# Feature-major projections: 640 tokens as 320 + 320 instead of 384 + 256

## The chip, the cores and the metric

The kernel runs on one core of one Trainium2 chip. The metric is the device time of one execution in microseconds (us): the median of three runs was 1576.16 us, with 1575.84 and 1576.3 as the lowest and highest.

## The reference, cut to what matters

Two layers act on 128 context tokens and 512 latent tokens, 640 rows of width 1024. Each layer has an input projection to 2560 columns, four mixers, an output projection, a layer norm, and a gated ConvFFN with a convolution of width 3 over the tokens.

```python
h = x * (1 + sc_a) + sh_a
qa, ka, va, ub, vb, qc, kc, vc, gcf, gcb, pd = project(h, w_in)
...
mix = jnp.concatenate([y_a, y_b, y_c, y_d], axis=-1) @ w_out
x = layer_norm(alpha * x + g_a * mix, ln_w[0], ln_b[0])
h = x * (1 + sc_f) + sh_f
x = layer_norm(alpha * x + g_f * conv_ffn(h, ffn_up, ffn_conv_w, ffn_conv_b, ffn_down), ln_w[1], ln_b[1])
...
def conv_ffn(h, up, cw, cb, down):
    u = h @ up
    up_ = jnp.pad(u, ((0, 0), (1, 1), (0, 0)))
    u = up_[:, :-2] * cw[0] + up_[:, 1:-1] * cw[1] + up_[:, 2:] * cw[2] + cb
    a, g = jnp.split(u, 2, axis=-1)
    return (jax.nn.silu(a) * g) @ down
```

## The kernel before, in words

The 640 tokens are five tiles of 128: t = 0 is the context, t = 1 to 4 are the latents. Every float32 operand of a large matmul is split into a high part (`hh` for activations, `wh` for weights) and a low part (`hl`, `wl`), and a product is three matmuls: wh·hh, wl·hh, wh·hl. ScalarE makes the high parts, VectorE subtracts to get the low ones.

Three kinds of projection follow from this.

- Feature-major (`fm_mms`, L537 to L550): 128 output features on the partitions, tokens along the free axis. One unit is one block of 128 features. A PSUM bank holds 512 float32 values, so the 640 tokens of a unit are two groups: `GA`, columns 0 to `SPLIT_COL`, and `GB`, the rest (L535). Each group takes 8 values of k by 3 matmuls, 24 in all. A layer has 16 units in the mixers (queries, keys, values of attention, `qc`, `kc`, gates, pool, `ub`) and 44 in the FFN's up-projection, so 120 units in the program.
- Token-major (`tm_mm`, L814 on) for two of the mixers' inputs: 256 columns a matmul. These don't use `SPLIT_COL`.
- Output and down projection (`wo`, `dn`): activations stationary, 512 columns of weights moving, one PSUM bank for each token tile.

The instructions of each engine stand in the order in which the program is written; there is no scheduler. So what stands at the head of an engine's queue holds up all behind it. The places that the prediction speaks of:

- Entry of the FFN (loop over `order`, L1424 on). The five GA groups of the first five units are issued first; the first GB follows when the queue of half-done units is longer than four. Between them stand the transposes of `to_h` (L508 on) for the last two token tiles: tile 3 after the second GA, tile 4 after the third. `to_h` makes `hh` and `hl` of one tile, in two halves of four k each: lower half L529 (ScalarE, hh) and L530 (VectorE, hl), upper half L531 and L532 (both VectorE). A GA group needs the tiles up to column `SPLIT_COL`; a GB group needs the others, down to the upper half of tile 4.
- The convolution on PSUM: `conv_a` for GA (ScalarE L1207, VectorE L1210 four times, L1213), `conv_b` for GB (ScalarE L1220, VectorE L1221, L1223, L1225).
- Entry of the mixers (`mixers`, L1057 on): four GA groups, four GB groups, each of the first three followed by `rope` on VectorE and GpSimd (L708 to L711), then the key splits (L580), both groups of the first `kc` unit, GA of the second, then `query_split` (L589, L590) and the first scores `sc` (L758), then GB of the second `kc` unit.
- Entry of the down projection (L1480 on): the first two k (`FIRST = 2`) are done for some token tiles ahead of the others, because `hh` and `hl` of the first four k (`EARLY = 4`) come in two parts: columns up to `SPLIT_COL` early, the rest (`early_rest`) after the last GB group.

Of the kernel before, what the change touches and what calls it, by code (L numbers as in the profile page):

```python
# [10 lines left out]
AF = mybir.ActivationFunctionType  # L11
# [3 lines left out]
P = 128  # L15
# [13 lines left out]

W = 640  # L30
NT = 5
SPLIT_COL = 384
UW = 664

C_ID, C_BD, C_MASK, C_RELF, C_TRIF, C_RELB, C_TRIB = 0, 128, 256, 896, 1024, 1152, 1280
# [54 lines left out]
def kernel(  # L90
# [6 lines left out]
    V, S, G, T = nc.vector, nc.scalar, nc.gpsimd, nc.tensor  # L97
# [18 lines left out]
    def unit(shape, name="u"):  # L116
        u = up.tile([P, UW], F32, tag="u", name=nm(name))[:, 0:math.prod(shape[1:])]
        if len(shape) == 3:
            u = u.rearrange("p (a b) -> p a b", b=shape[2])
        elif len(shape) == 4:  # L120
            u = u.rearrange("p (a b c) -> p a b c", b=shape[2], c=shape[3])
        return u
# [4 lines left out]
    def bank(n=512, name="m"):  # L127
        return pp.tile([P, 512], F32, tag="m", name=nm(name))[:, 0:n]
# [231 lines left out]
    def gate_tiles(a, gate, h):  # L360
        out = []
        for cnd in range(2):
            g = unit([P, 512], name="gate")
            side(out=g, in_=a.scratch[gate, cnd, h * 512:(h + 1) * 512].partition_broadcast(P))
            out.append(g)
        return out
# [14 lines left out]
    def params_tiles():  # L381
        return (par.tile([P, 38], F32, tag="prm", name=nm("prm")),
                par.tile([P, 4, 44], F32, tag="cwT", name=nm("cwT")))

    def params2(rc, prm, cwT):
        rows, cr = rc
        pt = bank(name="prT")
        T.transpose(pt[:, 0:38], rows[0:38, :], ident[0:38, 0:38])
        T.transpose(pt[:, 128:216], cr[0:88, 0, :], ident[0:88, 0:88])
        T.transpose(pt[:, 256:344], cr[0:88, 1, :], ident[0:88, 0:88])  # L390
        V.tensor_copy(out=prm, in_=pt[:, 0:38])
        V.tensor_copy(out=cwT[:, 0:2, :], in_=pt[:, 128:216].rearrange("p (t f) -> p t f", t=2))
        V.tensor_copy(out=cwT[:, 2:4, :], in_=pt[:, 256:344].rearrange("p (t f) -> p t f", t=2))
# [27 lines left out]
    def load_res(src, h, only=None, dma=None):  # L421
        for t in range(NT) if only is None else (only,):
            x = unit([P, 512], name="xr")
            (dma or side)(out=x, in_=src(t)[:, h * 512:(h + 1) * 512])
            xs[t, h] = x

    def gated(t, ps, gates):
        tmp = unit([P, 512], name="rt")
        V.tensor_tensor(out=tmp, in0=ps, in1=gates[cond_of(t)], op=ALU.mult)
        return tmp  # L430
# [33 lines left out]
    def normalize(t):  # L464
        r, nb = rn.pop(t)
        for h in range(2):
            S.activation(out=xs[t, h], in_=xs[t, h], func=AF.Identity, scale=r, bias=nb)
# [16 lines left out]
    def ln_bcast(l, i):  # L484
        out = []
        for src in (ln_w, ln_b):
            hs = []
            for h in range(2):
                u = unit([P, 512], name="lnb")
                side(out=u, in_=src[l, i, h * 512:(h + 1) * 512].partition_broadcast(P))  # L490
                hs.append(u)
            out.append(hs)
        return out

    def ln_scale(lnwb):
        for hs in lnwb:
            for u in hs:
                G.tensor_scalar(out=u, in0=u, scalar1=ALPHA, scalar2=None, op0=ALU.mult)
# [35 lines left out]

    GA, GB = (0, SPLIT_COL), (SPLIT_COL, W)  # L535

# [15 lines left out]
    def fm_mm(u, lo, hi):  # L552
        return fm_mms([u], lo, hi)[0]
# [434 lines left out]
    def pool_in(ps_a, ps_b):  # L988
        x = unit([P, 664], name="px")
        for a, b in ((0, 8), (136, 144), (656, 664)):  # L990
            G.memset(x[:, a:b], 0.0)
        S.activation(out=x[:, 8:136], in_=ps_a[:, 0:P], func=AF.Copy)
        S.activation(out=x[:, 144:400], in_=ps_a[:, P:SPLIT_COL], func=AF.Copy)
        S.activation(out=x[:, 400:656], in_=ps_b, func=AF.Copy)
        return x

    def pool_mix(m, prm, pt, x):
# [42 lines left out]
    def tick():  # L1040
        flush()
        if late:
            late.pop(0)()
        for ln in list(lanes):
            while ln:
                try:
                    next(ln[0])
                    break
                except StopIteration:
                    ln.pop(0)  # L1050
                    if ln:
                        continue
                    break
            if not ln:
                lanes.remove(ln)

    def mixers(l, m, prm, mid=None, then=None):  # L1057
# [8 lines left out]
        def start_a(*ii, mid=None, then=None):  # L1066
# [5 lines left out]
            for i, ps in zip(ii, pss):  # L1072
                S.activation(out=raws[i][:, 0:SPLIT_COL], in_=ps, func=AF.Copy)

        def start_b(i):
            ps = fm_mm(us[i], *GB)
            S.activation(out=raws[i][:, SPLIT_COL:W], in_=ps, func=AF.Copy)
            if i < 3:
# [28 lines left out]
        def keep(o):  # L1107
            u = ws.take()
            ps = fm_mm(u, *GA)
            S.activation(out=o[:, 0:SPLIT_COL], in_=ps, func=AF.Copy)  # L1110
            tick()
            ps = fm_mm(u, *GB)
            V.tensor_copy(out=o[:, SPLIT_COL:W], in_=ps)
            ws.free()
# [235 lines left out]
    for l in range(DEPTH):  # L1350
# [106 lines left out]
        def prep(i):  # L1457
            if i < len(steps):
                k = steps[i][1]
                act_split(k, 0, W)  # L1460
# [4 lines left out]
        def dmm(ps, t, k):  # L1465
            c0 = tcol(t)
            wh, wl = us[k // 2]
            s_ = k % KD
            T.matmul(ps, hh[:, s_, c0:c0 + P], wh[:, k % 2, :], start=(k == 0), stop=False)  # L1469
            T.matmul(ps, hh[:, s_, c0:c0 + P], wl[:, k % 2, :], start=False, stop=False)  # L1470
            T.matmul(ps, hl[:, s_, c0:c0 + P], wh[:, k % 2, :], start=False, stop=(k == KF - 1))  # L1471

        for h in range(2):
            pss = [bank(name="dn") for _ in range(NT)]
            us = {}
            cut = KF if h == 0 else KF - TAIL
            for k in range(KF):
                if k % 2 == 0:
                    us[k // 2] = ws.take()
                if k >= cut or k < FIRST - 1:  # L1480
                    continue
                if k == FIRST - 1:
                    for ts in (range(3), range(3, NT)):
                        for kk in range(FIRST):
                            for t in ts:
                                dmm(pss[t], t, kk)
                else:
                    for t in range(NT):
                        dmm(pss[t], t, k)
                if h == 0 and k == KF - 1:  # L1490
                    tmps = [gated(t, pss[t], gates) for t in range(2)] + [None] * 3
                if k % 2 == 1:
                    ws.free()
                while done < min(len(steps), h * KF + k + 1 + AHEAD):
                    prep(done)
                    done += 1
                if h == 1 and owed:
                    owed.pop(0)()
                if h == 1 and k == 7 and nxt:
                    prm2, cwT2 = params_tiles()  # L1500
                    params2(rc, prm2, cwT2)
                if h == 1 and k == 9:
                    gates = gate_tiles(adas[l], 1, 1)
                    load_res(lambda t, x=xd: x[t], 1)
                if h == 1 and k == 11:
                    lnb = ln_bcast(l, 1)
                if h == 1 and k == cut - 1 and nxt:
                    ln_scale(lnb)
            while h == 1 and done < len(steps):
                prep(done)  # L1510
                done += 1
            if h == 0:
                owed = [lambda t=t, ps=pss[t], g=gates, x=tmps[t]: resid(t, 0, ps, g, True, x) for t in range(NT)]
                owed.pop(0)()
                owed.pop(0)()
                continue
            for t in range(NT):
                for k in range(cut, KF):
                    dmm(pss[t], t, k)
                    if nxt and k == cut + 1:  # L1520
                        if t > 1:
                            to_h(t - 2, sb)
                        if t > 0:
                            normalize(t - 1)
                resid(t, 1, pss[t], gates, True)
                if nxt:
                    norm(t)
                else:
                    norm_out(t, lnb, y_out)
                if t == NT - 1:  # L1530
                    ws.free(4)
# [33 lines left out]
```

## Time and profile before

| What | Value |
|---|---|
| Median of three runs | 1576.16 us |
| The profiled execution | 1575.2 us, of which 1573.4 us are its span |
| Matmuls on TensorE | 1535.4 us busy, 98% of the span |
| Weight loads on TensorE | 1353.3 us, 86% |
| VectorE | 962.5 us, 61% |
| ScalarE | 618.0 us, 39% |
| GpSimd | 423.3 us, 27% |
| Mean granted clock of TensorE | 0.991 of full speed |

Busy time of TensorE is no measure of how near it is to its limit, since matmuls are pipelined and one is entered as longer than the distance to the next. The distance from start to start in the timeline is what one more matmul costs. The time of the profiled execution is 0.96 us below the median of the runs.

### The profile page before, as it was taken

The page shows a single profiled execution, that of the slowest core. Times are in us where ns is not written, and L with a number is a line of the kernel's source. Part 1 is how long each engine was busy: PE and PEld are TensorE (multiplying, and loading weights), DVE is VectorE, ACT ScalarE, POOL GpSimd, SP SyncE. Part 2 cuts the span into 40 slices and gives each one's busy share as a digit, 9 for nine tenths or more (in the row PEclk, how much of TensorE's full clock was granted, in tenths as well). Part 3 has the DMA queues.
Part 4 walks back from the last instruction along what each step waited for, and adds up shares of the span by engine and source line. Part 5 has one row for each costly group of instructions (what it writes and reads, how often), then busy time and mean ns, then how long its engine had stood idle before and what let it go on. Part 6 is the DMA issues. An engine that isn't in the chain of part 4 may idle for free.

```text
span 1573.4 us, 24493 instructions
## 1 busy us (share of the span) xinstructions
PE 1535.4 (98%) x9708; PEld 1353.3 (86%) x9708; DVE 962.5 (61%) x1864; ACT 618.0 (39%) x994; POOL 423.3 (27%) x486
## 2 busy tenths in 40 slices
PE   6999999999999999999997999999999999999997
PEld 1988868899999999988787898688999999997885
DVE  3775355786556555745578853657866656674456
ACT  2644453343333333533345344624433333343331
POOL 2402266054101101201127313732541101010104
PEclk9999999999999999999999999999999999999999
DMA  9544416145343443334215323161332221224311
GB/s 336 161 161 151 138 54 201 59 143 187 114 155 114 156 137 132 114 110 132 89 57 180 137 78 107 55 201 55 121 108 81 81 80 55 81 83 139 125 43 67
DMA packets 117791, 187.99 MB, mean 119 GB/s; under 512 B 11492, under 2 KB 77854, under 8 KB 117677
## 3 DMA queue, kind: packets, MB, share of 16 engines
q1 hardware_dynamic: 109517, 163.03, 31.1%
q0 software_dynamic: 8160, 23.40, 4.8%
q8 instruction: 76, 1.25, 0.3%
q14 instruction: 38, 0.31, 0.1%
HBM read 175.35 MB, written 11.04 MB: 118 GB/s over the span
## 4 chain that ended last, share of the span: by engine, by line
PE 88%; DVE 4%; POOL 3%; DMA 2%; issue 1%; ACT 1%; SPq 0%; POOLq 0%; ACTq 0%; DVEq 0%
PE fm L547 18%; PE fm L549 17%; PE fm L548 17%; PE dn L1470 6%; PE dn L1471 6%; PE dn L1469 6%; PE ada L233 2%; PE wo L1379 2%; PE wo L1381 2%; PE wo L1380 2%; DMA st<-in_w_ada_dram 1%; PE PT L794 1%; PE po L809 1%; PE tm L819 1%; PE tm L821 1%
## 5 line engine op out<-in xcount | busy, mean ns | idle before, releaser
L547 PE MATMUL fm<-hh,wh 128*128 128x256 f32 (+1 forms) x1920 | 601.0, 313 | 1.6 <-ACT hh L1299 1.6
L549 PE MATMUL fm<-hl,wh 128*128 128x256 f32 (+1 forms) x1920 | 594.5, 310 | 2.9 <-DVE hl L1304 2.0
L548 PE MATMUL fm<-hh,wl 128*128 128x256 f32 (+1 forms) x1920 | 594.0, 309 | 0.0
L246 DVE TENSOR_TENSOR wl<-st,wh 128x1024 fp32r<-128x1024 f32 x186 | 282.8, 1527 | 178.5 <-ACT wh L245 177.8
L547 PEld LDWEIGHTS fm<-hh,wh 128*128 128x128 f32 x1920 | 363.2, 189 | 30.4 <-ACT cv L1220 11.7
L549 PEld LDWEIGHTS fm<-hl,wh 128*128 128x128 f32 x1920 | 362.6, 189 | 4.8 <-DVE hl L1304 3.0
L548 PEld LDWEIGHTS fm<-hh,wl 128*128 128x128 f32 x1920 | 363.0, 189 | 0.1
L245 ACT ACTIVATE wh<-st 128x1024 fp32r<-128x1024 f32 x188 | 196.3, 1053 | 211.4 <-PE dn L1470 141.9
L1210 DVE SCALAR_TENSOR_TENSOR cv<-fm,cwT,cv 128x127 f32<-128x127 f32 x352 | 122.0, 408 | 109.5 <-ACT cv L1207 109.4
L1470 PE MATMUL dn<-wl,hh 128*128 128x512 f32 x440 | 175.1, 398 | 0.0
L1469 PE MATMUL dn<-wh,hh 128*128 128x512 f32 x440 | 173.7, 395 | 0.0
L1471 PE MATMUL dn<-wh,hl 128*128 128x512 f32 x440 | 173.1, 394 | 0.3 <-DVE hl L1406 0.2
L1207 ACT ACTIVATE cv<-fm,cwT 128x384 f32<-128x384 f32 x88 | 58.9, 673 | 204.2 <-PE fm L549 188.6
L1419 POOL TENSOR_TENSOR act<-cv,cv 128x640 f32<-128x640 f32 x28 | 45.6, 1630 | 301.2 <-DVE cv L1225 233.6
L1220 ACT ACTIVATE cv<-fm,cwT 128x255 f32<-128x255 f32 x88 | 49.6, 564 | 175.9 <-PE fm L549 175.9
L1471 PEld LDWEIGHTS dn<-wh,hl 128*128 128x128 f32 x440 | 82.6, 188 | 20.8 <-DVE hl L1406 1.1
L1469 PEld LDWEIGHTS dn<-wh,hh 128*128 128x128 f32 x440 | 82.6, 188 | 20.8
L1470 PEld LDWEIGHTS dn<-wl,hh 128*128 128x128 f32 x440 | 82.6, 188 | 19.1
L1419 POOL TENSOR_TENSOR y<-cv,cv 128x640 f32<-128x640 f32 x16 | 26.8, 1678 | 182.8 <-DVE cv L1225 182.8
L1221 DVE SCALAR_TENSOR_TENSOR cv<-fm,cwT,bnd 128x1 f32<-128x1 f32 x88 | 19.1, 217 | 89.1 <-ACT cv L1220 89.0
L1379 PE MATMUL wo<-wh,hh 128*128 128x512 f32 x160 | 64.6, 404 | 0.0
L450 POOL TENSOR_TENSOR r<-ve,mhalf 128x1 f32<-128x1 f32 x20 | 16.5, 826 | 177.4 <-DVE neg L456 177.1
(290 smaller groups left out, 2083.9 us busy)
## 6 DMA issues: line engine op xcount, KB each, us to landing
st<-in_ffn_up_dram SPq DMA_DIRECT2D x44, 1024.0 KB
wa<-in_w_ada_dram SPq DMA_DIRECT2D x80, 512.0 KB
st<-in_ffn_down_dram SPq DMA_DIRECT2D x88, 256.0 KB
st<-in_w_in_dram SPq DMA_DIRECT2D x20, 1024.0 KB
st<-in_w_ada_dram SPq DMA_DIRECT2D x16, 512.0 KB
xd<-xr SPq DMA_DIRECT2D x30, 256.0 KB
xr<-xd POOLq DMA_DIRECT2D x30, 256.0 KB, 5.6
st<-in_w_out_dram SPq DMA_DIRECT2D x24, 256.0 KB
```

The lines of the kernel that those rows point to most:

```text
L245: S.activation(out=oh, in_=view, func=AF.Copy)
L246: eng.tensor_tensor(out=ol, in0=view, in1=of, op=ALU.subtract)
L547: T.matmul(ps, wh[:, k, :], hh[:, k, lo:hi], start=(k == 0), stop=False)
L548: T.matmul(ps, wl[:, k, :], hh[:, k, lo:hi], start=False, stop=False)
L549: T.matmul(ps, wh[:, k, :], hl[:, k, lo:hi], start=False, stop=(k == KD - 1))
L1207: S.activation(out=o[:, 0:n], in_=ps, func=AF.Identity, scale=cwT[:, 1, f:f + 1], bias=cwT[:, 3, f:f + 1])
L1210: V.scalar_tensor_tensor(out=o[:, a + d:b - 1 + d], in0=ps[:, a + 1 - d:b - d], scalar=cwT[:, tap, f:f + 1], in1=o[:, a + d:b - 1 + d], op ...
L1379: T.matmul(ps, hh[:, k, c0:c0 + P], wh[:, k % 2, :], start=(k == 0), stop=False)
L1419: G.tensor_tensor(out=dst, in0=a, in1=g, op=ALU.mult)
L1469: T.matmul(ps, hh[:, s_, c0:c0 + P], wh[:, k % 2, :], start=(k == 0), stop=False)
L1470: T.matmul(ps, hh[:, s_, c0:c0 + P], wl[:, k % 2, :], start=False, stop=False)
L1471: T.matmul(ps, hl[:, s_, c0:c0 + P], wh[:, k % 2, :], start=False, stop=(k == KF - 1))
```

## The change: what it does, and the diff

`SPLIT_COL` becomes 320. Every GA and GB group is then 320 columns wide; 960 matmuls each of L547, L548 and L549 lose 64 columns and 960 each gain 64. The instructions on PSUM change in the same way: copies, gates, `conv_a` (its latent piece has 192 columns instead of 256) and `conv_b` (320 instead of 256). Token tile 2, columns 256 to 384, now lies in both groups. So the down projection takes two token tiles first instead of three, since only tiles 0 and 1 are complete in the early part. The pool mixer's copies get their columns from `SPLIT_COL`.

```diff
-SPLIT_COL = 384
+SPLIT_COL = 320
...
         S.activation(out=x[:, 8:136], in_=ps_a[:, 0:P], func=AF.Copy)
-        S.activation(out=x[:, 144:400], in_=ps_a[:, P:SPLIT_COL], func=AF.Copy)
-        S.activation(out=x[:, 400:656], in_=ps_b, func=AF.Copy)
+        S.activation(out=x[:, 144:16 + SPLIT_COL], in_=ps_a[:, P:SPLIT_COL], func=AF.Copy)
+        S.activation(out=x[:, 16 + SPLIT_COL:656], in_=ps_b, func=AF.Copy)
...
-                    for ts in (range(3), range(3, NT)):
+                    for ts in (range(2), range(2, NT)):
```

No instruction is added or removed on any engine. On TensorE, at the entry of layer 1's FFN, the end of the fifth GA group (`fm_10857`) and the start of the first GB group (`fm_10896`) before:

```order
L548 MATMUL fm_10857<-hh,wl_10660 128x384
L549 MATMUL fm_10857<-hl,wh_10659 128x384
L547 MATMUL fm_10896<-hh,wh_10337 128x256
L548 MATMUL fm_10896<-hh,wl_10338 128x256
L549 MATMUL fm_10896<-hl,wh_10337 128x256
```

And the same place of the changed kernel, on TensorE:

```order
L548 MATMUL fm_10857<-hh,wl_10660 128x320
L549 MATMUL fm_10857<-hl,wh_10659 128x320
L547 MATMUL fm_10896<-hh,wh_10337 128x320
L548 MATMUL fm_10896<-hh,wl_10338 128x320
L549 MATMUL fm_10896<-hl,wh_10337 128x320
```

Nothing moved there; only the widths differ. The one move is on TensorE at the entry of the down projection, here of layer 0 (`dn_6677` to `dn_6681` are the banks of token tiles 0 to 4):

```order
 L1470 MATMUL dn_6678<-wl_6395,hh 128x512
 L1471 MATMUL dn_6678<-wh_6394,hl 128x512
-L1469 MATMUL dn_6679<-wh_6394,hh 128x512
-L1470 MATMUL dn_6679<-wl_6395,hh 128x512
-L1471 MATMUL dn_6679<-wh_6394,hl 128x512
 L1469 MATMUL dn_6677<-wh_6394,hh 128x512
 L1470 MATMUL dn_6677<-wl_6395,hh 128x512
```

The three matmuls of k = 0 for token tile 2 now stand behind those of k = 1 for tiles 0 and 1, so 12 matmuls come ahead of the first that needs the late part, where it was 18.

## Rows read from the trace of the kernel before

**Rows 1.** The page: busy time of the engines; the chain that ended last.

```profile
PE 1535.4 (98%) x9708; PEld 1353.3 (86%) x9708; DVE 962.5 (61%) x1864; ACT 618.0 (39%) x994; POOL 423.3 (27%) x486
...
PE 88%; DVE 4%; POOL 3%; DMA 2%; issue 1%; ACT 1%; SPq 0%; POOLq 0%; ACTq 0%; DVEq 0%
```

**Rows 2.** Groups of instructions by shape, TensorE: count, busy us and mean ns, idle.

```profile
L547 PE MATMUL fm<-hh,wh 128*128 128x384 f32 x960 | 328.7, 342 | 1.6 <-ACT hh L1299 1.6
...
L547 PE MATMUL fm<-hh,wh 128*128 128x256 f32 x960 | 272.3, 284 | 0.0
```

**Rows 3.** Timeline, TensorE, one up-projection unit of layer 0: start us, us, instruction, [idle before].

```profile
455.05 0.28 PE L547 MATMUL fm<-hh,wh 128*128 128x256 f32 x1
...
457.90 0.34 PE L547 MATMUL fm<-hh,wh 128*128 128x384 f32 x1
...
462.07 0.28 PE L547 MATMUL fm<-hh,wh 128*128 128x256 f32 x1
```

**Rows 4.** Timeline, TensorE, the down projection of layer 0, 24 matmuls apart.

```profile
689.89 0.39 PE L1469 MATMUL dn<-wh,hh 128*128 128x512 f32 x1
...
695.49 0.39 PE L1469 MATMUL dn<-wh,hh 128*128 128x512 f32 x1
```

**Rows 5.** Timeline, TensorE, the first GA groups of layer 0, five matmuls apart.

```profile
42.38 0.52 PE L549 MATMUL fm<-hl,wh 128*128 128x384 f32 x1
...
43.98 0.44 PE L548 MATMUL fm<-hh,wl 128*128 128x384 f32 x1
```

**Rows 6.** Stretches: us, busy us (count) of each engine, granted clock, DMA share, GB/s.

```profile
860.00:864.00 4.00, 0.00 (x0) 0.00 (x0) 3.91 (x4) 2.98 (x7) 3.92 (x3) 0.50 0.72 289
...
866.20:870.20 4.00, 4.00 (x20) 4.00 (x20) 3.94 (x7) 0.00 (x0) 3.84 (x4) 0.50 0.17 66
...
34.00:44.20 10.20, 6.61 (x20) 4.99 (x19) 9.86 (x18) 9.70 (x20) 10.17 (x11) 0.50 0.97 311
```

**Rows 7.** Timeline, TensorE, entry of layer 1's FFN: the first GB group.

```profile
1119.77 0.28 PE L547 MATMUL fm<-hh,wh 128*128 128x256 f32 x1
...
1122.46 0.38 PE L549 MATMUL fm<-hl,wh 128*128 128x256 f32 x1 [0.87 <-DVE hl L532]
...
1123.74 0.34 PE L547 MATMUL fm<-hh,wh 128*128 128x384 f32 x1
```

**Rows 8.** Timeline, VectorE, the same entry: the last token tile.

```profile
1118.42 0.86 DVE L530 TENSOR_TENSOR hl<-h,hh 128x512 fp32r<-128x512 f32 x1 [0.70 <-ACT hh L529]
...
1120.76 1.65 DVE L532 TENSOR_TENSOR hl<-h,hh 128x512 fp32r<-128x512 f32 x1
```

**Rows 9.** Groups by shape, VectorE: the two shapes of conv_a's L1210.

```profile
L1210 DVE SCALAR_TENSOR_TENSOR cv<-fm,cwT,cv 128x255 f32<-128x255 f32 x176 | 83.2, 473 | 0.0
L1210 DVE SCALAR_TENSOR_TENSOR cv<-fm,cwT,cv 128x127 f32<-128x127 f32 x176 | 60.5, 344 | 109.5 <-ACT cv L1207 109.4
```

**Rows 10.** Timeline, TensorE, entry of layer 0's FFN: the first GB group.

```profile
341.93 0.28 PE L547 MATMUL fm<-hh,wh 128*128 128x256 f32 x1
...
343.59 0.28 PE L549 MATMUL fm<-hl,wh 128*128 128x256 f32 x1
...
344.78 0.34 PE L547 MATMUL fm<-hh,wh 128*128 128x384 f32 x1
```

**Rows 11.** Timeline, VectorE, the same entry: the last token tile.

```profile
339.10 0.97 DVE L530 TENSOR_TENSOR hl<-h,hh 128x512 fp32r<-128x512 f32 x1 [0.70 <-ACT hh L529]
...
341.54 1.67 DVE L532 TENSOR_TENSOR hl<-h,hh 128x512 fp32r<-128x512 f32 x1
```

**Rows 12.** Timeline, TensorE, the first scores of layer 1.

```profile
864.40 0.58 PE L758 MATMUL sc<-kh,qs 128*128 128x256 f32 x1 [8.21 <-DVE qs L590]
```

**Rows 13.** Timeline, VectorE, entry of layer 1's mixers: first rope, and the query split.

```profile
836.45 0.74 DVE L708 STREAM_SHUFFLE sw<-y 128x512 f32<-128x512 f32 x1
...
863.23 3.49 DVE L590 TENSOR_TENSOR qs<-y,qs 64x256 fp32r<-64x256 f32 x2
```

**Rows 14.** Timeline, TensorE, entry of layer 0's down projection.

```profile
664.35 0.50 PE L1471 MATMUL dn<-wh,hl 128*128 128x512 f32 x1
```

## The prediction

> **What bounds the kernel now.** I read the page first. TensorE is busy for 98% of the span and holds 88% of the chain that ended last, while VectorE, the next, is busy for 61% and holds 4% [rows 1]. So the time is the sum of TensorE's start-to-start distances plus the few places where it waits. The groups by shape say how much of it the change touches: 960 matmuls at each width for each of the three lines, so 5760 in 120 units [rows 2]; their busy times don't add up to the span, since neighbours overlap. The timeline has the real price. One GB group of 24 takes 457.90 - 455.05 = 2.85 us, 118.75 ns a matmul, and one GA group 462.07 - 457.90 = 4.17 us, 173.75 ns [rows 3]. A unit is 7.02 us.
>
> Then I looked for the waits of TensorE that lie next to a feature-major group. Three matter: the first GB group of layer 1's FFN, where one matmul waits for VectorE's last `hl` [rows 7], the same place in layer 0, where nothing waits [rows 10], and the first scores of layer 1, with 8.21 us of idle time [rows 12].
>
> **The spacing at 320 columns.** No row shows it. The nearest rows bound it at 118.75 ns (256 wide) and 173.75 ns (384 wide). Between them the question is whether the distance is proportional to the columns. Two groups speak for it. At full clock the 512-wide matmuls come at (695.49 - 689.89) / 24 = 233.3 ns [rows 4], 0.456 ns a column; at 384 it is 0.452, at 256 it is 0.464. And at the granted clock of 0.50 five 384-wide matmuls take 1.60 us, 320 ns each [rows 5, 6], which is 384 columns at 1.2 GHz with nothing on top. So I take 256 as the one that is a little dear for its width, and 320 at the rate of 384: 173.75 x 320 / 384 = 144.8 ns. A group is then 3.475 us and a unit 6.95 us, 0.07 us less. GA saves 0.695 us a unit, GB costs 0.625 us. Over 120 units this would be 8.4 us if nothing else bound: 6.16 us in the two FFNs (88 units) and 1.12 us in the mixers of each layer (16 units).
>
> The Trainium skill, "TensorE: Matmul & The Clock Gate", section "Back-to-back issue gap", gives the warm distance as N / 2.4 + 2.5 ns, a fixed cost plus a slope. By it two groups of 320 would take exactly what 384 and 256 take, and the unit would gain nothing. The estimates that it gives for 256 and 384 columns, 109 and 162.5 ns, lie below the 118.75 and 173.75 ns of this trace, and grow slower with the width; what a fixed part would do here is the first rival, worked out from rows.
>
> **Entry of the FFN.** Five GA groups run ahead of the first GB. They become 5 x 0.695 = 3.475 us shorter, so TensorE comes to the first GB 3.475 us earlier, and `hl` of the last token tile doesn't. In layer 1 that tile ends on VectorE at 1120.76 + 1.65 = 1122.41, with VectorE busy and only handing to ScalarE in between [rows 8]. What is ahead of it there gets a bit shorter: a `conv_a` has two ops of 255 columns, 473 ns, which become 191 wide; against 127 columns at 344 ns that is 1.0 ns a column, 0.13 us for each `conv_a` and 0.26 us for the two ahead [rows 9]. So `hl` ends at about 1122.15. The 15th matmul of the group needs it, the tenth from the end: 1122.15 + 0.05 + 10 x 0.1448 = 1123.65. Without the wait the group, started at 1119.77 - 3.475 = 1116.29, would end at 1119.77. The wait is 3.88 us; before it was 1123.74 - 1119.77 - 2.85 = 1.12 us [rows 7]. Added: 2.76 us.
>
> In layer 0 `hl` ends at 341.54 + 1.67 = 343.21 [rows 11], 0.38 us before the matmul that needs it, at 343.59 [rows 10]. After: 343.21 - 0.26 + 0.05 + 1.45 = 344.45 for the end of the group, against 341.93 - 3.475 + 3.475 = 341.93 without a wait. Added: 2.52 us. So the FFNs together keep 6.16 - 2.76 - 2.52 = 0.88 us. All matmuls queued behind the waiting one on TensorE wait with it. The price runs from nothing (VectorE's chain is that much faster once GpSimd's work falls elsewhere: the upper half's subtraction takes 1.65 us there) to the same again if that chain slips.
>
> **Entry of the mixers.** In layer 0 sixteen units save 1.12 us. The first 17 matmuls run at the granted clock of 0.50 and partly behind ScalarE and VectorE [rows 6], so I take 0.35 us of it back: 0.75 us. In layer 1 TensorE is idle before the first scores, so what its groups before them take doesn't count. The scores follow `query_split`, which starts on VectorE at 863.23; VectorE and GpSimd are in one chain from the first rope at 836.45 on [rows 13], and that starts when GB of the first unit is there. Four GA groups before it are 4 x 0.695 = 2.78 us shorter, but GB again waits for the last tile of `to_h`; I reckon that the chain starts 1.0 us earlier (bounds: 0 and 2.2 us, the saving less GB's growth). The 256-wide copy on VectorE becomes 320 wide: 0.07 us. After the scores the clock is still 0.50, to 870.2 [rows 6]. GB of the second `kc` unit runs in it, and costs 24 x 64 / 1.2 = 1.28 us more instead of 0.625; half of the 1.0 us, 0.5 us, is lost to the clock, which runs at half for so much longer. The ten units after it save 0.7 us. Together: -1.0 + 0.07 + 1.28 + 0.5 - 0.7 = +0.15 us. The stretch at 0.50 now covers 5.8 us of work after the scores; fallen at the start of the idle time, 856.2, it would cover 2.0 us, at its end 10.2 us, so this term can go about 2 us either way.
>
> **The rest.** The down projection now waits for the late part after 12 matmuls, 12 x 0.233 = 2.8 us, instead of 4.2 us. The one wait there today is at 664.35, at the 33rd matmul [rows 14], so other work of VectorE is late, not this part. I take 0.1 us off for the two layers; if the late part were short of time, it would cost up to the 1.4 us each by which the cover shrinks. The convolution's columns are only moved between `conv_a` and `conv_b`: VectorE and ScalarE do the same sum, under TensorE's groups of 3.475 us; if this cover went, as at the entry, it would show as waits on PSUM banks. The DMAs and the order of the weight splits don't change.
>
> **Sum.** -0.88 - 0.75 + 0.15 - 0.10 = -1.6 us. The profiled execution, 1575.2 us, becomes 1573.6 us; its median stands 0.96 us higher, so 1574.6 us.
>
> **The rivals.**
>
> 1. A fixed cost in the spacing. A line through 118.75 and 173.75 ns gives 146.25 ns at 320 columns and 228.8 ns at 512, 4.5 ns under [rows 4], where proportion to 384 gives 231.7 ns, 1.6 ns under; so the rows lean to proportion, but not by much. Then GA saves 0.66 us, GB costs 0.66 us, and no unit gains. Entry: layer 1 reaches GB at 1116.47, would end at 1119.98, ends at 1122.20 + 1.46 = 1123.66, so 3.68 - 1.12 = 2.56 us; layer 0 ends at 344.46 instead of 342.14, 2.32 us; mixers +0.35 in layer 0 and -1.0 + 0.07 + 1.28 + 0.5 = +0.85 in layer 1. The total is +6.1 us, 1582.3 us: slower. It decides from about 145.8 ns a matmul on, since each ns costs near 5 us.
> 2. The clock falls at the new waits. A stretch of 10.2 us at 0.50 follows thin work at 34.0 [rows 6], and the idle time before the scores brought one too. In layer 1 TensorE would be idle for most of 1116.3 to 1122.2. A fall there costs half of 10.2 us less what is waited for anyway, (10.2 - 3) / 2 = 3.6 us: 1578.2 us, and about 1581.8 us with both layers. Against it: the wait is in three pieces with matmuls between, and the 1.12 us of today brings none.
> 3. The entry doesn't hold. If `hl` is there when GB asks, both FFNs keep 6.16 us, and layer 1 also its 1.12 us: 1576.16 - 7.3 - 0.7 = 1568.2 us. For it speaks only that VectorE's three last steps are stretched by GpSimd's work [rows 8, 11], against it that they must gain 3 us in 6.
> 4. The change does nothing of what its widths say: a 320-wide matmul goes at the 384 price. That is 5760 x (173.75 - 146.25) = 158 us slower; nothing in the rows speaks for it.
>
> **How the numbers follow.** The main case has 0.60, its own range 1571 to 1578 us; rival 1 0.12, rival 2 0.14, rival 3 0.12, the fourth 0.02. About 0.2%, 3.15 us, is what can be told from no change. Faster by that (under 1573.0): rival 3 and a third of the main case, 0.32. Slower (over 1579.3): rivals 1 and 4, a third of rival 2, 0.19 with the rest of rounding. Within: 0.49. The range reaches half into the outer cases, 1569 to 1580.5 us.
>
> **What would show it.** Right: GA and GB groups of 3.47 us each in the timeline; at the first GB of each FFN waits of about 3.9 and 2.5 us with `hl` L532 as releaser; the first scores about 1 us earlier. Wrong: groups of 3.51 us (rival 1), a stretch of 0.50 clock near 1117 to 1130 (rival 2), no L532 wait (rival 3).

## The result, and the profile after

The changed kernel takes 1583.88 us (median of four runs, 1583.18 to 1584.58) against 1576.23 us of the kernel before in the same session (1575.84 to 1576.72). The ratio is 1.0051, with a 95% interval of 1.0037 to 1.0065: it is slower, by half a per cent. The forecast of 1574.6 us missed by 9.3 us, and its range, 1569 to 1580.5 us, doesn't hold the time. The nearest case was the first rival, at 1582.3 us.

The profiled execution has a span of 1581.4 us, 8.0 us longer than before. The page of the changed kernel, busy time and the chain that ended last:

```profile
PE 1540.9 (97%) x9708; PEld 1356.3 (86%) x9708; DVE 963.3 (61%) x1864; ACT 616.9 (39%) x994; POOL 422.3 (27%) x486
...
PE 83%; DVE 6%; POOL 4%; DMA 2%; ACT 2%; issue 2%; SPq 0%; POOLq 0%; ACTq 0%; DVEq 0%
```

Beside [rows 1], TensorE's busy time has risen by 5.5 us with the same 9708 matmuls, and its share of the chain has fallen from 88% to 83%: there is more matmul time and also more waiting. The two are read apart in the next views. First the groups by shape, changed kernel (count | busy us, mean ns | idle us and what ended it):

```profile
L547 PE MATMUL fm<-hh,wh 128*128 128x320 f32 x1920 | 601.7, 313 | 3.1 <-ACT hh L1299 1.5 <-ACT hh L529 1.4
...
L549 PE MATMUL fm<-hl,wh 128*128 128x320 f32 x1920 | 595.3, 310 | 4.9 <-DVE hl L532 2.2 <-DVE hl L1304 1.9 <-DVE hl L530 0.9
```

All 5760 are 320 wide now, so the change does what it says. L547's busy time is 601.7 us where the two widths of [rows 2] had 328.7 + 272.3 = 601.0 us: nothing is saved. And L532, the last `hl`, is waited for 2.2 us instead of 0.9.

The spacing stands in the timeline, TensorE, one unit of layer 0 (start us, us, instruction), the rows that answer to [rows 3]:

```profile
363.24 0.31 PE L547 MATMUL fm<-hh,wh 128*128 128x320 f32 x1
...
366.76 0.31 PE L547 MATMUL fm<-hh,wh 128*128 128x320 f32 x1
...
370.28 0.31 PE L547 MATMUL fm<-hh,wh 128*128 128x320 f32 x1
```

GB and GA take 3.52 us each, 146.7 ns a matmul. GA has become 0.65 us shorter and GB 0.68 us longer. From the start-to-start distances without rounding (medians of the groups 118.6 and 173.6 ns before, 146.67 after) a pair, one matmul of GA and one of GB, went from 292.2 to 293.3 ns, so a unit of 24 pairs is 0.03 us longer, and 120 units are 3.2 us longer. The forecast had them 8.4 us shorter.

The entry of layer 1's FFN, TensorE (in square brackets: idle time before, and what ended it), beside [rows 7]:

```profile
1120.74 0.31 PE L549 MATMUL fm<-hl,wh 128*128 128x320 f32 x1
...
1122.48 0.41 PE L547 MATMUL fm<-hh,wh 128*128 128x320 f32 x1 [1.43 <-ACT hh L529]
...
1123.47 0.41 PE L549 MATMUL fm<-hl,wh 128*128 128x320 f32 x1 [0.43 <-DVE hl L530]
...
1126.59 0.42 PE L549 MATMUL fm<-hl,wh 128*128 128x320 f32 x1 [1.09 <-DVE hl L532]
...
1128.16 0.31 PE L547 MATMUL fm<-hh,wh 128*128 128x320 f32 x1
```

and VectorE there, beside [rows 8]:

```profile
1122.46 0.95 DVE L530 TENSOR_TENSOR hl<-h,hh 128x512 fp32r<-128x512 f32 x1 [0.70 <-ACT hh L529]
...
1124.87 1.66 DVE L532 TENSOR_TENSOR hl<-h,hh 128x512 fp32r<-128x512 f32 x1
```

The last `hl` ends at 1124.87 + 1.66 = 1126.53, and the matmul that needs it starts 0.06 us later. Three operands are late one after another now; `hh` and `hl` of L529 and L530 were not waited for before. The end of the group, 1128.16, is set by VectorE, as forecast. Layer 0's entry, TensorE, beside [rows 10], has the same picture, where nothing waited before; only the first of the three operands is late by less there, some 0.3 us:

```profile
338.76 0.42 PE L547 MATMUL fm<-hh,wh 128*128 128x320 f32 x1
...
339.76 0.42 PE L549 MATMUL fm<-hl,wh 128*128 128x320 f32 x1 [0.44 <-DVE hl L530]
...
342.87 0.41 PE L549 MATMUL fm<-hl,wh 128*128 128x320 f32 x1 [1.08 <-DVE hl L532]
...
344.44 0.31 PE L547 MATMUL fm<-hh,wh 128*128 128x320 f32 x1
```

The group ends at 344.44; the forecast for it was 344.45. That they meet so closely is luck: the FFN began 0.37 us earlier than before, and counted from there the end is 0.36 us later than forecast.

The start of the same matmul in both traces says where the 8.0 us arose:

| TensorE reaches | before | after | shift |
|---|---|---|---|
| layer 0 FFN, first GA | 317.92 | 317.55 | -0.37 |
| layer 0 down projection | 656.59 | 659.89 | +3.30 |
| layer 1 mixers | 814.25 | 817.36 | +3.11 |
| layer 1 first scores | 864.40 | 867.26 | +2.86 |
| layer 1 FFN, first GA | 1096.97 | 1101.13 | +4.16 |
| layer 1 down projection | 1408.64 | 1416.80 | +8.16 |
| end of the span | 1573.4 | 1581.4 | +8.0 |

Each FFN's up-projection costs 3.7 to 4.0 us, layer 1's mixers 1.05 us, the rest gives a little back. In the kernel of experiment 6, where only the FFNs have the new split, the two stages cost 3.68 and 4.27 us.

### The profile page after: what moved, and what is told of

It reads as the page before. It is cut to its first block, busy times and chain, and to the rows that moved or that the text cites. A ratio compares the mean times of both kernels' runs of the same rounds, so it can differ in the third digit from the quotient of the medians.

```text
span 1581.4 us, 24495 instructions
## 1 busy us (share of the span) xinstructions
PE 1540.9 (97%) x9708; PEld 1356.3 (86%) x9708; DVE 963.3 (61%) x1864; ACT 616.9 (39%) x994; POOL 422.3 (27%) x486
## 4 chain that ended last, share of the span: by engine, by line
PE 83%; DVE 6%; POOL 4%; DMA 2%; ACT 2%; issue 2%; SPq 0%; POOLq 0%; ACTq 0%; DVEq 0%
PE fm L547 16%; PE fm L549 16%; PE fm L548 16%; PE dn L1470 6%; PE dn L1471 6%; PE dn L1469 6%; PE ada L233 2%; PE wo L1379 2%; PE wo L1381 2%; PE wo L1380 2%; DMA st<-in_w_ada_dram 1%; ACT h L527 1%; PE tm L819 1%; PE po L809 1%; PE PT L794 1%
## 5 line engine op out<-in xcount | busy, mean ns | idle before, releaser
L547 PE MATMUL fm<-hh,wh 128*128 128x320 f32 x1920 | 601.7, 313 | 3.1 <-ACT hh L1299 1.5
L549 PE MATMUL fm<-hl,wh 128*128 128x320 f32 x1920 | 595.3, 310 | 4.9 <-DVE hl L532 2.2
L548 PE MATMUL fm<-hh,wl 128*128 128x320 f32 x1920 | 594.2, 309 | 0.0
L246 DVE TENSOR_TENSOR wl<-st,wh 128x1024 fp32r<-128x1024 f32 x186 | 285.5, 1542 | 175.9 <-ACT wh L245 175.6
L547 PEld LDWEIGHTS fm<-hh,wh 128*128 128x128 f32 x1920 | 362.4, 189 | 32.4 <-ACT cv L1220 12.6
L549 PEld LDWEIGHTS fm<-hl,wh 128*128 128x128 f32 x1920 | 362.1, 189 | 7.7 <-DVE hl L532 2.7
L548 PEld LDWEIGHTS fm<-hh,wl 128*128 128x128 f32 x1920 | 362.4, 189 | 0.1
L1469 PE MATMUL dn<-wh,hh 128*128 128x512 f32 x440 | 173.6, 395 | 0.0
L1471 PE MATMUL dn<-wh,hl 128*128 128x512 f32 x440 | 173.4, 394 | 0.0
L1220 ACT ACTIVATE cv<-fm,cwT 128x319 f32<-128x319 f32 x88 | 54.3, 617 | 237.4 <-PE fm L549 237.4
L1210 DVE SCALAR_TENSOR_TENSOR cv<-fm,cwT,cv 128x127 f32<-128x127 f32 x352 | 110.0, 373 | 57.6 <-ACT cv L1207 57.5
L1207 ACT ACTIVATE cv<-fm,cwT 128x320 f32<-128x320 f32 x88 | 54.0, 620 | 149.9 <-PE fm L549 138.6
```

What stands on the lines that cost most here:

```text
L246: eng.tensor_tensor(out=ol, in0=view, in1=of, op=ALU.subtract)
L547: T.matmul(ps, wh[:, k, :], hh[:, k, lo:hi], start=(k == 0), stop=False)
L548: T.matmul(ps, wl[:, k, :], hh[:, k, lo:hi], start=False, stop=False)
L549: T.matmul(ps, wh[:, k, :], hl[:, k, lo:hi], start=False, stop=(k == KD - 1))
L1210: V.scalar_tensor_tensor(out=o[:, a + d:b - 1 + d], in0=ps[:, a + 1 - d:b - d], scalar=cwT[:, tap, f:f + 1], in1=o[:, a + d:b - 1 + d], op ...
L1220: S.activation(out=ob[:, 1:n], in_=ps[:, 1:n], func=AF.Identity, scale=cwT[:, 1, f:f + 1], bias=cwT[:, 3, f:f + 1])
```

## The experiments

Two questions were open: what law the spacing follows (proportional to the columns, a fixed cost plus a slope, or steps of 128 columns), and how much of the loss is the entry.

**1. The spacing by itself.** A kernel that leaves out the whole computation of the reference and runs only series of 48 matmuls in the FFN's pattern, one width and column offset at a time:

```python
for r in range(reps):
    for k in range(KD):
        T.matmul(ps, wh[:, k, :], hh[:, k, lo:lo + n], ...)
        T.matmul(ps, wl[:, k, :], hh[:, k, lo:lo + n], ...)
        T.matmul(ps, wh[:, k, :], hl[:, k, lo:lo + n], ...)
```

> This kernel leaves out the whole computation: it runs only series of 48 matmuls of one width each, in the order wh.hh, wl.hh, wh.hl of the projections, and writes zeros. It measures the disputed cost by itself: the start-to-start distance at full granted clock against the number of moving columns. Theory A, a cost for each started block of 128 columns: N/2.4 + 4.44 ns for each started 128, from 173.3 ns at 384 and 146.7 at 320. It gives 133.3 at 288, 160.0 at 352, 173.3 at 384, 181.1 at 392, 191.1 at 416, 204.4 at 448, 217.8 at 480, 231.1 at 512, so a jump of 7.8 ns from 384 to 392 for 8 columns. Theory B, a straight line through 118.75 at 256 and 173.75 at 384: 132.5 at 288, 160.0 at 352, 177.2 at 392, 187.5 at 416, 201.3 at 448, 228.8 at 512. Theory C, a fixed 13.3 ns: 133.3 at 288, 160.0 at 352, 176.7 at 392, 186.7 at 416, 200.0 at 448, 226.7 at 512. The rate of 384 for all widths, on which the prediction stood: 130.3 at 288, 159.3 at 352, 177.4 at 392. Below 256 the distance should stop falling, near 118.5 ns, if the 256-wide group is held up by something else than its columns. If blocks are counted from the address and not from the start of the operand, 256 columns from column 64 on cost 4.4 ns more, and so do 384 from column 64 on.

Its timeline, TensorE, the first matmul of a series and of the next, 48 apart (320 twice, at column 0 and at column 320):

```profile
53.58 0.28 PE L137 MATMUL ps<-hh,wh 128*128 128x256 f32 x1
...
59.32 0.28 PE L137 MATMUL ps<-hh,wh 128*128 128x256 f32 x1
...
65.08 0.29 PE L137 MATMUL ps<-hh,wh 128*128 128x264 f32 x1
...
77.17 0.31 PE L137 MATMUL ps<-hh,wh 128*128 128x320 f32 x1
...
84.20 0.31 PE L137 MATMUL ps<-hh,wh 128*128 128x320 f32 x1
...
91.25 0.32 PE L137 MATMUL ps<-hh,wh 128*128 128x352 f32 x1
...
98.93 0.33 PE L137 MATMUL ps<-hh,wh 128*128 128x376 f32 x1
...
107.25 0.34 PE L137 MATMUL ps<-hh,wh 128*128 128x384 f32 x1
...
115.57 0.33 PE L137 MATMUL ps<-hh,wh 128*128 128x384 f32 x1
...
172.47 0.39 PE L137 MATMUL ps<-hh,wh 128*128 128x512 f32 x1
...
183.37 0.39 PE L137 MATMUL ps<-hh,wh 128*128 128x512 f32 x1
```

The 320-wide series take 7.03 and 7.05 us, 48 x 146.7 ns, the 352-wide one 7.68 us (160.0 ns), the 384-wide one 8.32 us (173.3 ns), and the second 256-wide one 65.08 - 59.32 = 5.76 us (120.0 ns). The means of one execution, at a granted clock of 1.00 and without the first two matmuls of a series:

| columns | 128 | 192 | 240 | 256 | 264 | 288 | 320 | 352 | 376 | 384 | 392 | 416 | 448 | 480 | 504 | 512 |
|---|---|---|---|---|---|---|---|---|---|---|---|---|---|---|---|---|
| ns | 111.7 | 111.6 | 112.0 | 120.0 | 120.0 | 131.6 | 146.67 | 160.0 | 173.2 | 173.33 | 177.3 | 188.4 | 202.8 | 216.8 | 226.7 | 226.7 |

The second series at 256, 384 and 512, from column 64, is the one listed; from column 0 they gave 119.7, 173.4 and 226.9 ns. The five widths 256, 320, 352, 384 and 512 lie on one line within 0.1 ns: 13.33 ns and the columns at 2.4 GHz (320 / 2.4 = 133.3). Proportion would be 144.4 ns at 320 from 384, and from 256 150.0 ns. Steps of 128 columns are out too: 392 costs 4.0 ns more than 384, not 7.8, and the offset 320 costs nothing. But no single law is shown: the other widths from 264 up lie off the line by -3.3 to +3.5 ns, with 264 at the price of 256, 376 at that of 384 and 504 at that of 512; from 392 to 480 proportion to 384 fits within 0.6 ns, and at 288 and from 392 to 448 theory B lies nearer than C. From 240 down the price no longer falls. What is shown is the price at each width, and at 320 it is not the proportional one.

**2. Another split, 352 and 288.** On the changed kernel:

```diff
-SPLIT_COL = 320
+SPLIT_COL = 352
```

> The changed kernel with groups of 352 and 288 columns. Theory A: 160.0 + 133.3 ns, the same unit as with 320 and 320, since both groups start three blocks; only TensorE comes to the first GB of each FFN 1.6 us later than with 320, so 2 x 1.6 us less waiting and 4 x 0.32 us a layer more or less through the four GB groups that are left over: 1579 to 1581.5 us. Theory B and C: the unit is that of 384 and 256 (292.5 ns for two matmuls), and only the waits at the two entries stay, some 0.9 and 1.5 us more than before: 1577.5 to 1579 us. Groups of 24 in the timeline: 3.84 and 3.20 us by A, 3.84 and 3.18 us by B.

1581.09 us, ratio 1.0033 (1.0020 to 1.0046) to 1576.1 us. Its timeline, TensorE, one unit of layer 0:

```profile
359.35 0.43 PE L547 MATMUL fm<-hh,wh 128*128 128x352 f32 x1
...
363.30 0.29 PE L547 MATMUL fm<-hh,wh 128*128 128x288 f32 x1
...
366.50 0.32 PE L547 MATMUL fm<-hh,wh 128*128 128x352 f32 x1
```

GB takes 366.50 - 363.30 = 3.20 us, 133.3 ns a matmul; the 352-wide group, without its start behind a slower instruction, 160.1 ns. The pair is 293.4 ns, as at 320 and 320 and as the line gives for two widths that lie on it (2 x 13.33 + 640 / 2.4 = 293.3). By itself 288 is off the line, at 131.6 ns; why it costs 1.7 ns more in the kernel was not followed up. The time lies in the range of theory A, whose jump behind 384 the first experiment doesn't have; the expectation for B and C had put the pair at the old unit's 292.5 ns, 0.9 ns too low. By the time stamps the two FFNs cost 2.1 and 2.9 us, together 5.0 us, all of the loss of the trace. Some 2.3 us of that are 1.1 ns on 2112 pairs. The rest are the entries, about 1.2 us in layer 0 and 1.5 us in layer 1 more than before: the first GB of layer 0 ends within 0.05 us of the kernel before, although five narrower GA groups were 1.6 us shorter.

**3. The split turned round, 256 and 384.** `SPLIT_COL = 256` on the changed kernel: the same two widths as before, so the spacing stays, but the short group goes first.

> The changed kernel with groups of 256 and 384 columns: the unit costs exactly what it did before, in the other order, so the spacing drops out and what is left is the order: TensorE comes to the first GB of each FFN 5 x 1.32 = 6.6 us earlier than before, and waits. If the entry works as the prediction put it, each FFN loses 5 to 5.5 us, and the mixers of layer 1 about 1 to 2.5 us through a wider group at the granted clock of 0.50: 1586 to 1590 us. If the entry costs nothing and the whole loss of the change is spacing, it stays at 1576 to 1578 us.

1588.37 us, ratio 1.0078 (1.0066 to 1.0091). Its groups come at 118.6 and 173.5 ns, as before; one unit of layer 0, TensorE:

```profile
362.01 0.34 PE L547 MATMUL fm<-hh,wh 128*128 128x384 f32 x1
...
366.17 0.28 PE L547 MATMUL fm<-hh,wh 128*128 128x256 f32 x1
...
369.02 0.34 PE L547 MATMUL fm<-hh,wh 128*128 128x384 f32 x1
```

So the 12 us are not spacing. By the time stamps the FFNs cost 4.4 and 6.0 us, near the 5 to 5.5 us expected of each, and layer 1's mixers 3.7 us, more than the 1 to 2.5 us expected; the rest gives 2.1 us back. The entry of layer 1's FFN, TensorE:

```profile
1124.47 0.69 PE L547 MATMUL fm<-hh,wh 128*128 128x384 f32 x1 [5.18 <-ACT hh L529]
```

and the waits of TensorE (us in total, times, longest):

```profile
PE fm L547 <- ACT hh L529: 7.9, 2, 5.2
...
PE ckT L595 <- DMA ckv<-in_cache_attn_k_dram: 3.3, 1, 3.3
```

The narrower GA is, the earlier TensorE asks for the last token tile. The second wait is of the same kind, in front of layer 1's mixers: there a DMA is early enough only as long as GA takes its time.

**4. One more GA group ahead of the first GB.** On the changed kernel, to give VectorE time:

```diff
-            while len(queue) > (4 if i < 5 else 2):
+            while len(queue) > (5 if i < 6 else 2):
```

> The changed kernel, in which six GA groups instead of five run ahead of the first GB at the entry of each FFN, so TensorE comes there one group, 3.5 us, later. If the waits for the last token tile's low part are what the entry costs (about 2.5 us in layer 0, 3.6 us in layer 1), 5 to 6 us go: 1578 to 1579.5 us, and no wait for L532 is left or one under 0.3 us. If the wait only moves, because six units' weights are then held and the next can't be split ahead, the time stays over 1582 us and a wait for wh or wl stands a little later.

1595.0 us, ratio 1.012 (1.0105 to 1.0136), the slowest of all. The wait for L532 is gone, and others take its place. Timeline, TensorE, at the two entries:

```profile
350.29 3.17 PE L233 MATMUL ada<-wa,scT 128*32 128x512 f32 x8 [4.11 <-DMA wa<-in_w_ada_dram]
...
1142.16 0.64 PE L548 MATMUL fm<-hh,wl 128*128 128x320 f32 x1 [3.89 <-DVE wl L246]
```

and the stretches around them (us, busy us of PE, PEld, DVE, ACT, POOL with counts, granted clock, DMA share, GB/s):

```profile
350.00:355.00 5.00, 3.89 (x10) 0.82 (x10) 1.23 (x1) 1.06 (x1) 0.15 (x1) 0.50 0.41 159
...
1140.00:1145.00 5.00, 2.84 (x11) 2.84 (x12) 2.07 (x3) 0.00 (x0) 0.71 (x1) 0.54 0.13 52
```

This is the expectation's second case. A sixth group holds one more unit's weights, and the kernel splits no further weights while six units' are held (`NW // 2`), so the next weights come late: their split on VectorE (L246) keeps TensorE 3.9 us, a weight DMA 4.1 us, and TensorE's clock falls to 0.50 at each. The fall that the second rival feared at the entry's three short waits comes here, at waits of about 4 us in one piece.

**5. The last tile's work one group earlier.** On the changed kernel, and as the same edit on the kernel before:

```diff
-            for _ in range(0 if i == 0 else 1 if i < 3 else 2):
+            for _ in range(0 if i == 0 else 2):
```

On the changed kernel:

> The changed kernel, with the last token tile's transposes and modulation put one unit earlier at the entry of each FFN, right behind those of tile 3, so VectorE makes its hl before the conv_a of the second unit (1.4 us) and in layer 0 before one weight split (2.1 us). If the waits for that hl are the entry's price, layer 0 loses its wait of 2.5 us and layer 1 1.4 of its 3.6 us: 1583.9 - 3.9 = 1580 us, between 1579 and 1581. If the wait moves to the PSUM bank of the second unit or to a late weight split, it stays over 1582.5 us.

1580.71 us, ratio 1.0030 (1.0019 to 1.0042) to 1575.86 us. Waits of TensorE:

```profile
PE fm L549 <- DVE hl L532: 1.1, 1, 1.1
...
PE fm L549 <- DVE hl L530: 0.6, 1, 0.6
PE fm L548 <- DVE wl L246: 0.5, 1, 0.5
```

and the end of the first GB in layer 0 and in layer 1, TensorE:

```profile
342.25 0.30 PE L547 MATMUL fm<-hh,wh 128*128 128x320 f32 x1
```

```profile
1124.87 0.31 PE L547 MATMUL fm<-hh,wh 128*128 128x320 f32 x1
```

Layer 0's first GB now ends at 342.25 without a wait, 2.2 us earlier than in the changed kernel; layer 1's at 1124.87 instead of 1128.16 still waits 1.1 us for L532. By the time stamps the FFNs cost 2.07 and 2.80 us instead of 3.67 and 4.00: 1.6 us are won in layer 0, where a wait of 0.5 us for a late weight split follows, and 1.2 us in layer 1. Layer 1's mixers, which the edit doesn't touch, take 0.6 us less in this trace. So about 2.8 of the 3.3 us by which the two traces differ were the entries', and the kernel is still slower than before. On the kernel before:

> The same move of the last tile in the kernel before, 384 and 256. Layer 0 has no wait there to lose, layer 1 has 1.1 us: 1575.0 us, 1.1 us less than before, which is under 0.2%. If the moved work delays the weight splits, it is slower than before by 1 us or more.

1574.8 us, ratio 0.9993 (0.9984 to 1.0002): not told apart from the kernel before, whose waits at these places add up to 1.1 us. In its trace the first GB of layer 1 wins 0.97 us (it ends 0.36 us later than in the kernel before, where it had been 1.33 us behind at the start of the FFN). The same move is worth about 1 us there and about 3 us with the new split, so the larger part of what it wins is a price of the change.

**6. The FFN alone.** 320 and 320 in the FFN, 384 and 256 in the mixers:

> Only the FFN is split 320 and 320 (up-projection, convolution, early parts and the first step of the down projection); the mixers keep 384 and 256. By the time stamps of the changed kernel its mixers cost 0.7 us in all (-0.4 in layer 0, +1.05 in layer 1), so 7 of its 7.7 us are the FFNs': 1583.2 us, 1582.5 to 1584. If the mixers cost more than they show there, because TensorE's idle time before the scores swallows or returns it, it is nearer to 1580 us.

```diff
+FS = 320
 ...
     def conv_a(cwT, f, ps):
-        n = SPLIT_COL
+        n = FS
```

1583.26 us, ratio 1.0048 (1.0036 to 1.0061), as expected. So 7.4 us of the loss are the FFNs', and what the mixers add (0.0048 against 0.0051) is less than these runs can tell.

**7. Why 256 is cheaper in the kernel.** There it comes at 118.6 ns, by itself at 120.0. A second kernel of matmuls alone, which again leaves out the reference's computation, runs groups of 24: one width throughout, 384 and 256 in turn, and the same weights or the same moving operand all the time.

> This kernel leaves out the whole computation and writes zeros: it runs groups of 24 matmuls alone, in the order of the projections. The scan of widths gave N/2.4 + 13.33 ns from 320 to 384 and 120.0 ns at 256, while the 256-wide groups inside the kernel before come at 118.5 ns. Here 384 (columns from 0) and 256 (columns from 384) alternate with changing weights, as in the kernel before, then 320 and 320. Theory 1, the alternation or the offset of 384 lets the 256-wide group run below its own price: 118 to 118.8 ns here. Theory 2, it is something else in the kernel (other engines, other addresses): 120.0 ns here too. 320 should stay at 146.7 ns at both offsets, 384 at 173.3. If the price above N/2.4 belongs to the change of weights, a group in which all three matmuls of a k load the same weights, or in which the moving operand is the same, could be cheaper; if it is a fixed cost of every matmul, all of these stay at 120.

Timeline, TensorE, a 256-wide group followed by a 384-wide one, and two groups of 320:

```profile
48.40 0.28 PE L141 MATMUL ps<-hh,wh 128*128 128x256 f32 x1
...
51.27 0.34 PE L141 MATMUL ps<-hh,wh 128*128 128x384 f32 x1
...
75.89 0.31 PE L141 MATMUL ps<-hh,wh 128*128 128x320 f32 x1
...
79.41 0.31 PE L141 MATMUL ps<-hh,wh 128*128 128x320 f32 x1
```

In turn with 384, 256 comes at (51.27 - 48.40) / 24 = 119.6 ns, 119.4 without rounding, which is between the two theories; 320 keeps 146.7 ns; repeated weights or a repeated operand leave 256 at 120.0, but each matmul has a weight load of its own in these series too (648 loads for 648 matmuls in this kernel), so whether the fixed part belongs to the load isn't shown. Only the first seven or so matmuls behind another width come closer, at 116 to 122 ns, and the rest at 120; in the kernel the distances keep changing between 115 and 122 ns through the whole group. So alternation explains about 0.6 of the 1.4 ns. The other 0.8 ns, about 2.3 us over 2880 matmuls and so most of the 3.2 us by which the units grew, stays open.

## Why the prediction was wrong

**The step that failed is "The spacing at 320 columns".** It took the distance as proportional to the columns, 144.8 ns, and it is 146.7 ns, in the kernel and by itself. With that one number put right, the sum for the FFNs goes from 0.88 us kept to 7.1 us lost (worked out at the end of this section), 7.9 of the 9.6 us between the forecast, 1.6 us shorter, and the trace, 8.0 us longer. Proportion was the mistake: by themselves two groups of 320 cost what 384 and 256 cost, 293.3 ns a pair, since all three widths lie on one line with a fixed part of 13.33 ns; in the kernel they cost 1.1 ns more, and neither 320 and 320 nor 352 and 288 gains. The two supports were weak ones. The 512-wide matmuls of [rows 4] come at 233.3 ns, but 512 by itself takes 226.7 ns, so in the down projection something else, which stays open, adds 6.6 ns; a price from another stage, with other neighbours, was taken for a point of the same line. And the 320 ns of [rows 5], at half clock, are 384 columns with nothing on top; that the fixed part isn't there at 0.50 says nothing of 1.00. The two rows that were of the kind in question, [rows 3], gave 146.25 ns by a straight line, and that was the first rival.

The Trainium skill, "TensorE: Matmul & The Clock Gate", section "Back-to-back issue gap", has a fixed cost plus a slope, by which the unit gains nothing, and the traces agree with that: 292.2 ns a pair before, 293.3 after. Its fixed cost of 2.5 ns isn't this kernel's: the line through the five widths has 13.33 ns beside the same slope.

**Entry of the FFN: right in its mechanism, its sizes partly by luck.** With GA 0.65 us shorter, layer 0's first GB would have ended at 341.83 (341.93 - 0.37 - 5 x 0.65 + 3.52) and ended at 344.44: 2.61 us added, 2.52 forecast. Layer 1's would have ended at 1124.20 (1119.77 + 4.16 - 3.25 + 3.52) and ended at 1128.16: a wait of 3.96 us (forecast 3.88), of which 1.12 us are old; 2.84 us added, 2.76 forecast. Two errors cancel in this. Counted from the FFN's first GA group, the last `hl` ended 0.02 us earlier than before in layer 0 and 0.04 us in layer 1, where 0.26 us was forecast, although `conv_a`'s wider op took 405 ns instead of 473, as forecast; so the group ended some 0.35 us later than forecast. And by the true spacing it would have ended 0.27 us later without any wait. VectorE's chain didn't get faster, so the third rival is out.

**The clock at the entries: right not to count it.** The stretches, changed kernel, with the waits of each entry in them:

```profile
1118.00:1129.00 11.00, 8.05 (x51) 7.26 (x51) 9.83 (x23) 4.18 (x10) 9.45 (x7) 1.00 0.23 89
...
336.00:345.00 9.00, 7.36 (x46) 6.57 (x46) 7.84 (x17) 3.92 (x9) 7.80 (x5) 1.00 0.75 230
```

The granted clock stays at 1.00 in both; the second rival didn't come.

**Entry of the mixers: sizes off.** Layer 0 gave 0.37 us instead of 0.75, but one trace can't tell this: kernels that are the same up to this place reach it up to 1.21 us later than the kernel before (384 and 256, experiments 5 and 6), or from 0.24 us earlier to 0.14 us later (320 and 320, experiments 5 and 4). In layer 1 the term was +0.15 and came out as +1.05 us (+1.46 and +0.44 us in experiments 4 and 5, which have the same mixers). The rope was to start 1.0 us earlier, and starts 0.23 us earlier (839.33 against 836.45 + 3.11), since two operands are late now that were not. The matmul ahead of the first unit's GB waits for a cache DMA, so ScalarE's copy `y` of that GB comes late, at 838.33 + 0.44 = 838.77; but the start of the rope is set by a buffer whose write-out is under way until 0.4 us later. Changed kernel, TensorE, ScalarE and then VectorE:

```profile
834.43 0.33 PE L595 MATMUL ckT<-ident,ckv 128*128 128x128 f32 x1 [0.87 <-DMA ckv<-in_cache_attn_k_dram]
```

```profile
838.33 0.44 ACT L1077 ACTIVATE y<-fm 128x320 f32<-128x320 f32 x1 [1.18 <-PE fm L549]
```

```profile
839.30 0.01 DVE L708 LOAD_MASK_SELECT sw<-y  x1 [1.52 <-DMA xd<-xr]
839.33 0.74 DVE L708 STREAM_SHUFFLE sw<-y 128x512 f32<-128x512 f32 x1
```

So the first scores gained 0.25 us and not 0.9. GB of the second `kc` unit, forecast at 1.28 us and 0.5 us of clock, cost 0.57 us together. The forecast took all of it as running at half clock, but even before only 18 of its 24 matmuls did (213 ns apart), and after 13 (267 ns apart): the granted clock is 0.68 there, changed kernel.

```profile
870.00:874.30 4.30, 4.30 (x23) 4.30 (x21) 4.24 (x7) 0.00 (x0) 4.22 (x3) 0.68 0.16 61
```

The units after it lost 0.73 us (shift from +3.43 to +4.16) instead of gaining 0.7: the spacing again for about 1.0 us of the difference; the rest was not followed up.

**The down projection: as forecast, small.** The wait at its 33rd matmul [rows 14] is gone in layer 0, and the shift falls by 0.2 us from there to the mixers of layer 1. Smaller cover for the late part cost nothing.

**What the sum would have been.** With 146.67 ns put right (beside 118.6 and 173.6 ns), and all else as forecast, the 88 units of the FFNs are +2.3 us instead of -6.16, and the entries 2.5 and 2.2 us instead of 2.76 and 2.52: +7.1 us in all. The stages measured +3.67 and +4.00, 7.7 us; the entries, measured at 2.84 and 2.61 us, are the difference. Most of what is left of the miss, 1.3 us, is in the mixers.

## What to carry to other kernels

Two widths don't give a law of the spacing: a rate taken through the origin hides a fixed cost per matmul, and with a fixed cost an even split gains nothing while the number of matmuls stays; the very width that the change needs, measured in the same pattern, decides it before anything is built on it. The 24 matmuls of a group are also the cover under which another engine finishes the next operand, so a shorter first group brings forward the moment at which TensorE asks; computed from the producer's last row, the end of the group held to 0.4 us here. A deeper queue ahead wasn't a remedy here, since it holds the weight buffers.

## What the runs showed of the hardware that was not expected

- At full clock a matmul with its own weight load costs its columns at 2.4 GHz and 13.33 ns more at 256, 320, 352, 384 and 512 columns (at 256 also when weights or operand repeat), while other widths from 264 up lie up to 3.5 ns off that line; at the granted clock of 0.50, 384 columns took 320 ns [rows 5], and 256 and 320 columns 213 and 267 ns, the columns at 1.2 GHz with no fixed part.
- From 240 columns down to 128 the spacing stays at 112 ns; 264 columns cost the same 120.0 ns as 256, 376 the same as 384 within 0.2 ns, and 504 the same 226.7 ns as 512.
- In turn with 384, 256-wide matmuls are 0.6 ns cheaper on average than 256 throughout, all of it in the first seven or so of a group; in the kernel they are 1.4 ns cheaper, the rest of it unexplained.
